# Attention's first query part and one head's rope rows ahead of the other rope copies; second-gate conditioning in the inverse stage, GpSimd out of it

## The chip, the cores and the metric

The kernel runs on one core of one Trainium2 chip. A core has a matrix engine (TensorE, PE in the rows, with its weight loads as PEld), VectorE (DVE), ScalarE (ACT), GpSimd (POOL) and SyncE (SP), which issues most DMA transfers. The metric is the device time of one execution in microseconds (us), as the median of several runs. All times below are microseconds unless a row says ns.

## The reference, cut to what matters

One step of a two-layer diffusion model on 1,024 latent tokens and 128 context tokens with 1,024 channels. Layer 0 mixes with a gated long convolution (Hyena), layer 1 with latent attention of 16 heads. Each layer adds gate * mixer output, and (shift, scale, gate) comes from the conditioning vector.

```python
def adaln(cond, w, b):                      # one call per layer and token group
    m = (jax.nn.silu(cond) @ w + b)[:, None, :]
    return jnp.split(m, 3, axis=-1)         # shift, scale, gate

def hyena_mix(h, ...):                      # layer 0
    proj = h @ w_in
    u = short_conv(proj[..., :3 * HY_WIDTH], conv_w, conv_b)
    gate = proj[..., 3 * HY_WIDTH:]
    x0, x1, v = jnp.split(u, 3, axis=-1)
    z = v * x1
    y = irfft(rfft(z) * hf)[:L]             # hf: the filters' spectrum
    y = (y + z * f_bias) * x0
    return (y * jax.nn.silu(gate)) @ w_out

def mla_latent(h, ...):                     # layer 1, latent tokens
    q_a, kv_a, k_pe, gate = split(h @ w_in)
    q = rmsnorm(q_a) @ w_qb                 # 64 plain and 32 rope columns a head
    ckv = rmsnorm(kv_a)
    q_pe, k_pe = rope(q_pe), rope(k_pe)     # k_pe is shared by all heads
    k_nope, v = split(concat(ckv, ckv_ctx) @ w_kvb)
    p = softmax((q_nope @ k_nope.T + q_pe @ k_pe.T) * scale)
    return ((p @ v) * jax.nn.silu(gate)) @ w_o

xs = xs + g_s * os_                         # the gate of each layer
```

## The kernel before, in words

Everything is fp32 in and out. A product that needs accuracy is made of three matmul passes: each operand is split into a high part (`hi`, a copy into the matmul's own format) and a low part (`lo`, the difference), and high*high, low*high and high*low are added. So `wi_h`/`wi_l`, `lhh`/`lhl` and `kT0`/`kT1` are high and low parts, and an argument of the helper says on which engine each is made.

The program is written stage by stage, and each engine executes its instructions in the order in which they stand in its own list. Blocks under `urgent` are put ahead of work that was written earlier and has not been placed yet; inside `issue_after(last)` work is placed behind a given instruction. The tile framework adds the waits, and a tile that takes over the space of an earlier one waits for that tile's readers. All transfers called on `nc.sync` are issued in order by SP, so one that waits holds up those behind it.

**The inverse stage.** The latent convolution is done by a discrete Fourier transform in eight groups of 128 channels. The inverse transforms (`inverse(g)`) read the spectra of each group with four `pi_raw` loads from PS, one `pp_raw` load (the context tokens), combine them on VectorE (`bf<-Z`, `bf<-ds`, `ds<-W`), and let TensorE transform back (line 548, tile `iv_ps`) into `yv`. In the same stage the last input projections run, for the gate path (`gate_group`, line 418, tile `ip_ps`): their weights come by `wi_raw` loads, their high part is made on ScalarE, and their low part `wi_l` on GpSimd. For the groups whose gate is ready, `gate_y` loads the gate (`xg`), multiplies `yv` by it, and the product is stored to YD. A string of steps, PLAN, sets how inverse transforms (I and i) and gate projections (g) are interleaved; I includes `gate_y`. YP and YG list the groups whose two products run on GpSimd. This work lies between 589 and 717 us after the start. Then `w_out` starts: it splits y into `lhh` and `lhl` and multiplies by the output weights (line 619, tile `wo_ps`).

**Conditioning.** `ada_chunk` loads 1 MB of conditioning weights for 256 columns, multiplies eight 128-row pieces with the conditioning vectors in four groups of rows of one PSUM tile, and copies them out on ScalarE (`ada_ev`). `ada_row` adds the four groups with a small product by `sel`, loads the bias row (`ada_row`), adds it on VectorE, and stores the result by a DMA that GpSimd issues, into `gate_rows`. Those of the second layer's gate are four calls, made after the last `mla_gate` and before `attend`, with their tiles in the space of the `mla_gate` weights and silu tiles (`like`). Their result is read at the end, in `mla_out`.

**The entry of attention.** `mla_gate` makes the attention gate with three-pass products and a silu each (`gsil`), and SP stores it. `attend` then makes the tiles `kT0`, `kT1`, `qT` and `Vt` in space that was freed, and fills the rope rows of `kT` for the four heads of a group from `krh`/`krl` by eight DMA copies (line 976), a row block of 64 each. `attention` then makes the key parts for the first pair (`k_proj`, products of line 989, as those of the query parts; the values are made in line 1021), calls `start(0)`, which loads the gate tile `gt` (two DMAs) and `rope_q`, and makes the three query parts. Part 0 holds the rope columns: its products are copied to `rot0`/`rot1` on ScalarE, 32-row blocks are swapped by two DMAs each (`rot<-rot`), and GpSimd multiplies by `rope_q` and writes `qT`. The scores (line 1287) follow.

Of the kernel before, what the change touches and what calls it, by code (L numbers as in the profile page):

```python
# [9 lines left out]
F32 = mybir.dt.float32  # L10
# [7 lines left out]
P = 128  # L18
D = 1024

GATES = (0, None, None, 1, None, None, None, None)
NY = 6
YP, YG = (0, 1), (0, 1, 2, 3, 4)
WT = ((0, 1, 2, 3), (4, 5), (6, 7), (8,))
XB = 4
PLAN = "g2 I0 I1 g3 I2 I3 g4 g5 I4 i5 i6 i7"
WRB = 3
# [11 lines left out]
GB = 2  # L39
HP = (0,)  # L40
W_LO = "dve"
# [34 lines left out]
class K:  # L76
# [27 lines left out]

    def ada_chunk(self, layer, o, n, pool, ps, kk, bufs, like=None):

        pt = ps.tile([P, 512], F32, name="ada_ps", tag=self.ada_tag, bufs=self.nada)[:, 0:n]
        for k in range(0, 8, kk):
            if like:
                w = pool.tile([P, 8, 336], F32, name="ada_w", tag=like, bufs=bufs)[:, :, 0:n]  # L110
            else:
                w = pool.tile([P, kk, n], F32, name="ada_w", tag="ada_w", bufs=bufs)
            self.ada_dma = self.nc.sync.dma_start(w, self.a["ada_w"][layer, o // 256][:, k:k + kk, o % 256:o % 256 + n])
            for i in range(kk):
                g = (k + i) % 4
                self.PE.matmul(pt[32 * g:32 * g + 32, :], self.cond[:, k + i, :], w[:, i, :],
                               start=k + i < 4, stop=k + i >= 4, tile_position=(0, 32 * g))
        ev = pool.tile([P, n], F32, name="ada_ev", tag="gsil" if like else "ada_ev", bufs=2 if kk * n > 1024 else 1)
        self.S.copy(ev, pt)
        return ev  # L120
# [19 lines left out]

    def ada_row(self, layer, gd, o, n, pool, ps, kk, bufs, like=None):

        ev = self.ada_chunk(layer, 2 * D + o, n, pool, ps, kk, bufs, like)
        pt = ps.tile([P, 512], F32, name="ada_ps", tag=self.ada_tag, bufs=self.nada)[:, 0:n]
        self.PE.matmul(pt[0:2, :], self.sel, ev, start=True, stop=True)
        row = pool.tile([P, n], F32, name="ada_row", tag="gsil", bufs=2)[0:2] if like else pool.tile([2, n], F32, name="ada_row", tag="ada_row", bufs=1)
        self.nc.sync.dma_start(row, self.a["ada_gb"][layer:layer + 1, o:o + n].squeeze(0).partition_broadcast(2))
        self.tt(row, row, pt[0:2, :], ALU.add)
        self.nc.gpsimd.dma_start(gd.squeeze(0)[:, o:o + n], row)
# [497 lines left out]
    def hyena(self):  # L647
# [107 lines left out]
        with self.pool("pc", side="right") as pc, self.pool("pb1", 1, side="right") as pool, \  # L755
# [10 lines left out]
            for step in PLAN.split():  # L766
                c, g = step[0], int(step[1])
                if c == "g":
                    with tc.issue_after(last):
                        self.gate_group(g, q)  # L770
                    late.append(g)
                else:
                    with self.urgent():
# [71 lines left out]
    def mla(self, lh, hT, lT, wp, wo, gd, AB):  # L845
# [3 lines left out]
        with self.pool("mcs", space=PSUM) as ps:  # L849
# [8 lines left out]
            with self.pool("mww", side="left") as wpool:  # L858
# [23 lines left out]
                for h in range(1, 4):  # L882
                    self.mla_gate(h, wpool, ps, hT, lT, GD, 2)
                    if h == 1:
                        self.load_kq(m, "wk", 0, "act", "dve")
                        self.load_kq(m, "wq", 0, "act", "dve")

                self.ada_tag, self.nada = "nm_ps", 3
                for o in range(0, D, 256):
                    self.ada_row(1, gd[1], o, 256, wpool, ps, 8, 2, "wm_" + "hl"[o // 256 % 2])  # L890
            lh.release()
# [72 lines left out]
    def attend(self, at, m):  # L964
# [6 lines left out]

        for j in (0, 2):
            r = slice(32 * j, 32 * j + 64)
            for x, y in zip(kT, m["kr"]):
                for i in range(2):
                    nc.sync.dma_start(x[r, j + i, :].bitcast(F32), y[r, :].bitcast(F32))

# [71 lines left out]
    def attention(self, m):  # L1049
# [20 lines left out]
        def now(work):  # L1070
            for g in work:
                for _ in g:
                    pass

        m["fin"] = None
        now(self.k_proj(m, 0, b) for b in range(3))
        cur, work = start(0)
        now(work)
        u = unit(cur, 0)
# [4 lines left out]
        with self.tc.manual_schedule(engines=ordered):  # L1084
            for G in range(4):
                for ci in range(4):
# [21 lines left out]
                    cur = nxt  # L1108
# [386 lines left out]
```

## Time and profile before

| | us |
|---|---|
| median of 3 runs | 1825.76 (1824.81 to 1826.91) |
| the profiled execution | 1825.55 |
| its span | 1823.7 |
| PE busy | 1753.8 (96%), 11,064 matmuls |
| DVE busy | 1256.7 (69%) |
| ACT busy | 1087.5 (60%) |
| POOL busy | 551.7 (30%) |

The profiled execution lies 0.2 below the median, and its span 1.9 below its own time; what lies around the span is taken as unchanged. Shares are of the whole span, over stages with different limits. A row of the timeline gives the start of a group of like instructions, the time from its first start to its last end, engine, line, operation, out<-in with the names of tiles, shape, count, and in brackets how long its engine sat idle before it and what ended that wait. L976 is line 976 of the kernel before. A row of the chain gives start, duration and what the time was spent on: an engine at work, a DMA, or SP's queue (SPq).

### The profile page before, as it was taken

What the parts mean: (1) busy time and instruction counts of PE and PEld (TensorE: products, weight loads), DVE (VectorE), ACT (ScalarE), POOL (GpSimd) and SP (SyncE); (2) the same over time, 40 slices, a digit from 0 to 9 for tenths busy, and PEclk for the clock granted to TensorE, in tenths of its full rate; (3) what the DMA queues carried; (4) which work ended last, traced back from release to release, by engine and by line L of the source; (5) the groups of instructions that cost most, each with busy time, mean ns of one, the idle gap of its engine ahead of it and who ended that gap; (6) DMA issues with size and microseconds to landing.
All of it is one profiled execution on the core that took longest, in us unless ns stands there. A gap on an engine that the chain in (4) does not pass through costs nothing.

```text
span 1823.7 us, 30675 instructions
## 1 busy us (share of the span) xinstructions
PE 1753.8 (96%) x11064; PEld 1575.4 (86%) x11064; DVE 1256.7 (69%) x2518; ACT 1087.5 (60%) x2580; POOL 551.7 (30%) x756
## 2 busy tenths in 40 slices
PE   6999999999999989999999799999999999999898
PEld 4888989989899878889999589999999999998786
DVE  3948787898885897442250387878787888778454
ACT  7655565756664224334451488878887888788332
POOL 2433333433444232331000143433423342344100
PEclk9999999999999989999999899999999999999999
DMA  8233332111133646323133410100000010002541
GB/s 324 91 110 109 112 104 72 50 54 49 57 102 111 204 154 260 129 82 101 43 92 114 127 32 23 39 24 24 28 30 28 20 32 21 25 29 67 185 133 70
DMA packets 98448, 157.87 MB, mean 87 GB/s; under 512 B 11703, under 2 KB 68311, under 8 KB 97016
## 3 DMA queue, kind: packets, MB, share of 16 engines
q1 hardware_dynamic: 95488, 152.51, 25.7%
q10 hardware_dynamic: 2552, 3.39, 0.6%
q8 instruction: 87, 1.43, 0.3%
q14 instruction: 65, 0.53, 0.1%
q0 software_dynamic: 256, 0.02, 0.0%
HBM read 113.89 MB, written 36.73 MB: 83 GB/s over the span
## 4 chain that ended last, share of the span: by engine, by line
PE 78%; DVE 9%; DMA 5%; ACT 3%; issue 3%; POOL 2%; SPq 1%; DVEq 0%; ACTq 0%; POOLq 0%
PE wo_ps L619 18%; PE ip_ps L418 14%; PE wo_ps L1287 12%; PE av_ps L1172 8%; PE nm_ps L1160 7%; PE wo_ps L989 5%; PE df_ps L367 3%; PE iv_ps L548 2%; PE nm_ps L1021 1%; DMA pi_raw<-PS 1%; DMA wi_raw<-w_in 1%; POOL wi_l L96 1%; DVE pr_o L99 1%; DVE mx L1290 1%; DVE cv L102 1%
## 5 line engine op out<-in xcount | busy, mean ns | idle before, releaser
L1287 PE MATMUL wo_ps<-kT,qT 128*128 128x512 f32 (+1 forms) x1152 | 281.2, 374 | 11.2 <-POOL qT L90 7.5
L1294 ACT ACTIVATE prob<-wo_ps,mx 128x512 f32<-128x512 f32 (+1 forms) x384 | 234.5, 619 | 22.7 <-DVE mx L1292 20.9
L1290 DVE TENSOR_REDUCE mx<-wo_ps 128x1 f32<-128x512 f32 (+1 forms) x384 | 213.0, 596 | 33.0 <-PE wo_ps L1287 32.4
L88 ACT ACTIVATE pt_h<-nm_ps 128x512 fp32r<-128x512 f32 x324 | 193.1, 600 | 70.5 <-PE nm_ps L1160 63.2
L1287 PEld LDWEIGHTS wo_ps<-kT,qT 128*128 128x128 f32 x1152 | 189.0, 190 | 46.5 <-ACT prob L1294 13.4
L96 DVE TENSOR_TENSOR pt_l<-nm_ps,pt_h 128x512 fp32r<-128x512 f32 x324 | 210.7, 683 | 13.0 <-ACT pt_h L88 12.9
L1160 PE MATMUL nm_ps<-ident,prob 128*128 128x128 f32 x1280 | 191.4, 272 | 0.0
L96 POOL TENSOR_TENSOR wi_l<-wi_raw,wi_h 128x512 fp32r<-128x512 f32 x64 | 111.8, 1747 | 242.8 <-ACT wi_h L88 234.6
L1160 PEld LDWEIGHTS nm_ps<-ident,prob 128*128 128x128 f32 x1280 | 150.0, 140 | 8.5
L418 PE MATMUL ip_ps<-hT,wi_h 128*128 128x384 f32 x720 | 152.8, 346 | 0.8 <-ACT cv L500 0.8
L418 PE MATMUL ip_ps<-lT,wi_h 128*128 128x384 f32 x720 | 153.2, 342 | 0.0
L418 PE MATMUL ip_ps<-hT,wi_l 128*128 128x384 f32 x720 | 152.1, 343 | 0.0
L1172 PE MATMUL av_ps<-pt_h,Vt 128*128 128x256 f32 x640 | 138.0, 297 | 0.3 <-ACT pt_h L88 0.3
L1172 PE MATMUL av_ps<-pt_l,Vt 128*128 128x256 f32 x640 | 135.5, 293 | 0.3 <-DVE pt_l L96 0.2
L418 PEld LDWEIGHTS ip_ps<-hT,wi_h 128*128 128x128 f32 x720 | 127.2, 191 | 6.3 <-issue 2.1
L418 PEld LDWEIGHTS ip_ps<-hT,wi_l 128*128 128x128 f32 x720 | 126.3, 189 | 6.8 <-issue 3.3
L418 PEld LDWEIGHTS ip_ps<-lT,wi_h 128*128 128x128 f32 x720 | 128.3, 190 | 3.4 <-issue 0.4
L619 PE MATMUL wo_ps<-wm_h,lhh 128*128 128x256 f32 (+1 forms) x432 | 125.8, 295 | 1.6 <-ACT wm_h L88 1.6
L619 PE MATMUL wo_ps<-wm_l,lhh 128*128 128x256 f32 (+1 forms) x432 | 126.9, 294 | 0.1
L619 PE MATMUL wo_ps<-wm_h,lhl 128*128 128x256 f32 (+1 forms) x432 | 127.0, 295 | 0.0
L1184 POOL TENSOR_SCALAR gt<-gt,sm 128x64 f32<-128x64 f32 x128 | 54.9, 443 | 225.2 <-DVE sm L1175 223.9
L99 POOL TENSOR_TENSOR pr<-ev 128x256 f32<-128x256 f32 x72 | 83.8, 1169 | 128.9 <-ACT ev L375 81.0
(338 smaller groups left out, 4096.7 us busy)
## 6 DMA issues: line engine op xcount, KB each, us to landing
wi_raw<-w_in SPq DMA_DIRECT2D x64, 256.0 KB, 2.9
ada_w<-ada_w SPq DMA_DIRECT2D x12, 1024.0 KB, 7.1
ada_w<-ada_w SPq DMA_DIRECT2D x24, 512.0 KB, 3.9
x_in<-xs SPq DMA_DIRECT2D x16, 512.0 KB, 5.9
PS<-pr_o SPq DMA_DIRECT2D x64, 128.0 KB, 1.9
pi_raw<-PS SPq DMA_DIRECT2D x32, 256.0 KB, 4.0
YD<-yv SPq DMA_DIRECT2D x8, 576.0 KB, 3.3
y<-YD SPq DMA_DIRECT2D x8, 576.0 KB, 10.3
```

The costliest lines, as they stand in the source:

```text
L88: self.S.activation(out, src, AF.Copy)
L96: e.tensor_tensor(out, src, hi.bitcast(F32), ALU.subtract)
L99: (eng or self.V).tensor_tensor(out, x, y, op)
L418: mm = self.PE.matmul(pt, w[:, k, :], x[c][:, k, :], start=s == 0 and k == 0, stop=s == 2 and k == 7)
L619: self.PE.matmul(pt, x[k][:, sl], w[:, k, :], start=s == 0 and k == 0, stop=s == 2 and k == kt - 1)
L989: self.PE.matmul(pt[:, :n], x[:, k, o:o + P], y[:, k, c], start=s == 0 and k == 0, stop=s == 2 and k == kt - 1)
L1160: self.PE.transpose(pt[:, P * i:P * i + P], u["p"][i % 2][n // 2][:, P * (2 * (n % 2) + i // 2):P * (2 * (n % 2) + i // 2) + P], self.ident)
L1172: self.PE.matmul(u["po"][:, :256], m["V"][:, 2 * n + e, j, :], u[n][1 + s][:, 256 * e:256 * e + 256], start=n == first and e + s == 0, sto ...
L1184: self.G.tensor_scalar(o, o, u["sm"][:, i, 3:4], None, ALU.mult)
L1287: self.PE.matmul(pt[:, :n], x[:, j, P * i:P * i + P], y[:, j, o:o + n], start=s == 0, stop=s == 2)
L1290: self.V.tensor_reduce(mx[:, b:b + 1], c["s", i, b][:, :n], AX.X, ALU.max)
L1294: self.S.activation(c["p"][i][b], c["s", i, b][:, :n], AF.Exp, bias=c["mx"][i][:, 3:4], accum_out=c["sm"][:, i, b:b + 1])
```

## The change

Four things are done. The second layer's gate conditioning (the four `ada_row` calls) moves from the space between `mla_gate` and `attend` into PLAN, as the steps a0 to a3, with tiles of the inverse stage's own pool, and the option `like` goes. The lists YP, YG and HP become empty: the five products `yv*xg`, two low parts `lhl` and one high part `lhh` that GpSimd made are now made by VectorE (the `lhh` by ScalarE). In `attend` the rope rows of head 0 (j=0) are written by a VectorE cast (kT1 by ScalarE), and the other three by DMA copies: six instead of eight. In `attention`, `start(0)` and query part 0 are issued under `urgent`, ahead of the first keys in the code.

```diff
-YP, YG = (0, 1), (0, 1, 2, 3, 4)
+YP, YG = (), ()
-PLAN = "g2 I0 I1 g3 I2 I3 g4 g5 I4 i5 i6 i7"
+PLAN = "g2 I0 a0 I1 g3 I2 a1 I3 g4 a2 g5 I4 a3 i5 i6 i7"
-HP = (0,)
+HP = ()
...
-    def ada_chunk(self, layer, o, n, pool, ps, kk, bufs, like=None):
+    def ada_chunk(self, layer, o, n, pool, ps, kk, bufs):
...
-            if like:
-                w = pool.tile([P, 8, 336], F32, name="ada_w", tag=like, bufs=bufs)[:, :, 0:n]
-            else:
-                w = pool.tile([P, kk, n], F32, name="ada_w", tag="ada_w", bufs=bufs)
+            w = pool.tile([P, kk, n], F32, name="ada_w", tag="ada_w", bufs=bufs)
...
@@ inverse stage
+                elif c == "a":
+                    self.ada_row(1, gd[1], 256 * g, 256, pool, ps, 8, 2)
...
@@ mla(), after the last mla_gate
-                self.ada_tag, self.nada = "nm_ps", 3
-                for o in range(0, D, 256):
-                    self.ada_row(1, gd[1], o, 256, wpool, ps, 8, 2, "wm_" + "hl"[o // 256 % 2])
...
@@ attend()
-        for j in (0, 2):
-            r = slice(32 * j, 32 * j + 64)
-            for x, y in zip(kT, m["kr"]):
-                for i in range(2):
-                    nc.sync.dma_start(x[r, j + i, :].bitcast(F32), y[r, :].bitcast(F32))
+        for j in (0, 2, 1, 3):
+            r = slice(64 * (j // 2), 64 * (j // 2) + 64)
+            for i, (x, y) in enumerate(zip(kT, m["kr"])):
+                x, y = x[r, j, :], y[r, :].bitcast(F32)
+                if j:
+                    nc.sync.dma_start(x.bitcast(F32), y)
+                elif i:
+                    self.S.copy(x, y)
+                else:
+                    self.V.tensor_copy(x, y)
...
@@ attention()
+        with self.urgent():
+            cur, work = start(0)
+            now(work[:1])
         now(self.k_proj(m, 0, b) for b in range(3))
-        cur, work = start(0)
-        now(work)
+        now(work[1:])
```

SP's list at the entry of attention, before. `ada_w` and `ada_row` are the loads of the last second-gate chunks, `krh` and `krl` the split rope rows, `gate0` and `gate1` the stored attention gate, `rot0` the first half of query part 0:

```order
L113 DMA ada_w_10319<-ada_w 128x8x256
L147 DMA ada_row_10295<-ada_gb 2x256
L147 DMA ada_row_10314<-ada_gb 2x256
L147 DMA ada_row_10333<-ada_gb 2x256
L147 DMA ada_row_10352<-ada_gb 2x256
L976 DMA kT0_10361<-krh_9350 64x1408 x2
L976 DMA kT1_10362<-krl_9351 64x1408 x2
...
L1061 DMA gt_10413<-gate0_7332 128x256
L1061 DMA gt_10413<-gate1_7333 128x256
L1063 DMA rope_q_10416<-rope_q 128x256
L1042 DMA rot0_10428<-rot0_10428 32x256 x2
```

The "..." stands for the second set of four copies. The same place on SP in the changed kernel, from the last two gate stores on; the "..." stands for the second and third pair of copies:

```order
L957 DMA gate7_7415<-gsil_10325 128x256
L957 DMA gate8_7416<-gsil_10353 128x256
L972 DMA kT0_10361<-krh_9426 64x1408
L972 DMA kT1_10362<-krl_9427 64x1408
...
L1061 DMA gt_10380<-gate0_7408 128x256
L1061 DMA gt_10380<-gate1_7409 128x256
L1063 DMA rope_q_10383<-rope_q 128x256
L1042 DMA rot0_10395<-rot0_10395 32x256 x2
```

The conditioning loads have left the place, the copies stand directly behind the last gate store, two copies are gone, and the gate tile, `rope_q` and the swaps are still behind all copies.

SP's list in the inverse stage, before, from the third group's loads on (PS2 and PS3 are the spectra of groups 2 and 3, XG1 the gate of group 1, YD0 the product of group 0):

```order
L591 DMA pp_raw_6151<-PP2_90 128x256
L402 DMA wi_raw_7048<-w_in 128x512
L544 DMA pi_raw_6095<-PS2_82 128x2x256
L544 DMA pi_raw_6103<-PS2_82 128x2x256
L544 DMA pi_raw_6111<-PS2_82 128x2x256
L544 DMA pi_raw_6119<-PS2_82 128x2x256
L591 DMA pp_raw_6219<-PP3_91 128x256
L599 DMA xg_5901<-XG1_97 128x1152
L778 DMA YD0_104<-yv_5803 128x1152
L544 DMA pi_raw_6163<-PS3_83 128x2x256
```

The same place in the changed kernel:

```order
L588 DMA pp_raw_6170<-PP2_90 128x256
L110 DMA ada_w_6454<-ada_w 128x2048
L541 DMA pi_raw_6114<-PS2_82 128x2x256
L399 DMA wi_raw_7124<-w_in 128x512
L541 DMA pi_raw_6122<-PS2_82 128x2x256
L144 DMA ada_row_6194<-ada_gb 2x256
L541 DMA pi_raw_6130<-PS2_82 128x2x256
L777 DMA YD0_104<-yv_5803 128x1152
L596 DMA xg_5920<-XG1_97 128x1152
L541 DMA pi_raw_6138<-PS2_82 128x2x256
L588 DMA pp_raw_6257<-PP3_91 128x256
L110 DMA ada_w_6728<-ada_w 128x2048
```

A 1 MB load of conditioning weights stands ahead of the third group's spectra, the bias row's load between them, and the store of group 0 and the gate load of group 1 have moved ahead of that group's last load.

GpSimd's list over the inverse stage, before (`yv` with its gate `xg`, the low parts `wi_l` of the last gate projections, and `lhh`/`lhl` of the output projection):

```order
L96 TENSOR_TENSOR wi_l_6953<-wi_raw_6958,wi_h_6952 128x512
L99 TENSOR_TENSOR yv_5803<-yv_5803,xg_5833 128x1152
L99 TENSOR_TENSOR yv_5871<-yv_5871,xg_5901 128x1152
L99 TENSOR_TENSOR yv_6126<-yv_6126,xg_6156 128x1152
L99 TENSOR_TENSOR yv_6194<-yv_6194,xg_6224 128x1152
L96 TENSOR_TENSOR wi_l_7047<-wi_raw_7048,wi_h_7046 128x512
...
L99 TENSOR_TENSOR yv_6636<-yv_6636,xg_6666 128x1152
...
L90 TENSOR_SCALAR lhh0_7296<-y0_6874 128x1152
L96 TENSOR_TENSOR lhl0_7297<-y0_6874,lhh0_7296 128x1152
L96 TENSOR_TENSOR lhl1_7301<-y1_6875,lhh1_7300 128x1152
```

And in the changed kernel:

```order
L96 TENSOR_TENSOR wi_l_7029<-wi_raw_7034,wi_h_7028 128x512
L146 DMA gate_rows1_907<-ada_row_5852 2x256
L146 DMA gate_rows1_907<-ada_row_6194 2x256
L146 DMA gate_rows1_907<-ada_row_6468 2x256
L96 TENSOR_TENSOR wi_l_7123<-wi_raw_7124,wi_h_7122 128x512
L96 TENSOR_TENSOR wi_l_7123<-wi_raw_7128,wi_h_7122 128x512
L146 DMA gate_rows1_907<-ada_row_6742 2x256
L96 TENSOR_TENSOR wi_l_7216<-wi_raw_7217,wi_h_7215 128x512
```

The five products and three splits are gone from GpSimd; the `wi_l` splits stay, and the four stores of conditioning rows stand among them.

## Rows read from the trace of the kernel before

**Rows 1.** The page's chain that ended last, share of the span by engine.

```profile
PE 78%; DVE 9%; DMA 5%; ACT 3%; issue 3%; POOL 2%; SPq 1%; DVEq 0%; ACTq 0%; POOLq 0%
```

**Rows 2.** Windows: stretch, sum, PE PEld DVE ACT POOL busy, PEclk, DMA share, GB/s.

```profile
1030.00:1040.00 10.00, 4.85 (x12) 3.56 (x12) 2.05 (x4) 0.00 (x0) 5.90 (x10) 0.55 0.32 94
```

**Rows 3.** Timeline of all engines from 995 us on, the last gate store.

```profile
1000.19 0.61 SPq L962 DMA_DIRECT2D gate<-gsil  x1
```

**Rows 4.** The chain in order of time, 1000 to 1060 us.

```profile
1000.63 4.40 PE wo_ps L989 x21
...
1014.16 0.55 SPq L976
...
1020.27 2.15 SPq L976
...
1022.46 1.52 SPq L976
...
1030.65 2.05 DMA rot<-rot
...
1040.88 1.32 PE wo_ps L1287 x6
```

**Rows 5.** Timeline of PE, 1012 to 1056 us.

```profile
1011.64 1.11 PE L116 MATMUL ada_ps<-ada_w,cond 128*32 128x256 f32 x13
...
1013.78 0.51 PE L1021 MATMUL nm_ps<-wk_h,ckh 128*128 128x256 f32 x2
...
1017.00 0.62 PE L989 MATMUL wo_ps<-qnh,wq_h 128*128 128x256 f32 x3 [0.33 <-DVE kT L96]
...
1034.13 4.85 PE L1287 MATMUL wo_ps<-kT,qT 128*128 128x512 f32 x12 [7.50 <-POOL qT L90]
```

**Rows 6.** Timeline of DVE, 596 to 732 us.

```profile
608.96 3.19 DVE L99 TENSOR_TENSOR bf<-Z 128x256 f32<-128x256 f32 x2
...
660.61 4.12 DVE L99 TENSOR_TENSOR bf<-ds 128x256 f32<-128x256 f32 x2
...
667.31 0.76 DVE L99 TENSOR_TENSOR bf<-Z 128x256 f32<-128x256 f32 x2
...
670.33 1.83 DVE L99 TENSOR_TENSOR ds<-W 128x768 f32<-128x768 f32 x2 [2.26 <-ACT W L549]
...
718.87 1.35 DVE L96 TENSOR_TENSOR lhl<-y,lhh 128x1152 fp32r<-128x1152 f32 x1
```

**Rows 7.** Timeline of POOL, 596 to 732 us.

```profile
608.98 2.88 POOL L99 TENSOR_TENSOR yv<-yv,xg 128x1152 f32<-128x1152 f32 x1 [7.62 <-ACT yv L594]
...
652.30 9.40 POOL L96 TENSOR_TENSOR wi_l<-wi_raw,wi_h 128x512 fp32r<-128x512 f32 x1 [6.45 <-ACT wi_h L88]
...
702.47 2.10 POOL L90 TENSOR_SCALAR lhh<-y 128x1152 fp32r<-128x1152 f32 x1 [8.60 <-PE ip_ps L418]
```

**Rows 8.** Timeline of PE, 638 to 735 us.

```profile
665.92 3.75 PE L548 MATMUL iv_ps<-ic,pi_raw 128*128 128x256 f32 x8 [5.00 <-DMA pi_raw<-PS]
...
717.66 0.50 PE L619 MATMUL wo_ps<-wo_h,lhl 128*128 128x512 f32 x1 [1.51 <-DVE lhl L96]
```

**Rows 9.** Timeline of ACT, 596 to 732 us.

```profile
716.38 1.16 ACT L88 ACTIVATE lhh<-y 128x1152 fp32r<-128x1152 f32 x1 [0.88 <-DVE y L99]
```

**Rows 10.** The chain in order of time, 590 to 735 us.

```profile
681.20 29.51 PE ip_ps L418 x170
```

**Rows 11.** Tile ada_ps: count: duration ns min/median/max, first and last start us, forms.

```profile
L145 PE MATMUL ada_ps<-ada_ev,sel x16: 377/378/378, 95.7 to 1013.5; 128*2 128x256 f32 x16
```

**Rows 12.** Tile ada_row, the columns as above.

```profile
L99 DVE TENSOR_TENSOR ada_row<-ada_row,ada_ps x8: 396/404/409, 96.4 to 1015.2; 2x256 f32<-2x256 f32 x8
L149 POOL DMA_DIRECT2D gate_rows<-ada_row x8: 518/552/756, 97.5 to 1015.9; - x8
...
DMA to landing us min/median/max: 1.6/3.1/4.6
```

**Rows 13.** The DMA view, 595 to 690 us.

```profile
DMA packets 10476, 15.61 MB, mean 164 GB/s; under 512 B 787, under 2 KB 8523, under 8 KB 10468
```

## What the change should do: the prediction

> **What bounds the kernel now.** I read the page first: the chain of work that ended last is TensorE for 78% [rows 1], so an edit is worth what it takes out of the stretches in which TensorE waits. The windows show two such stretches where the diff works: the inverse stage (about 590 to 717 us) and the entry of attention (1000 to 1046 us).
>
> At the entry, the store behind the last gate silu is issued at 1000.19 for 0.61 [rows 3]. The first score matmul starts at 1034.13, after 7.50 us in which TensorE waits for a GpSimd row of qT [rows 5]. The chain in order of time says why: it runs through the queue of SP. The first kT copy goes out at 1014.16, the seventh of eight at 1022.46, then gt, rope_q and the rot swaps follow, and the first swaps land at 1032.70, 2.05 after 1030.65 [rows 4]. The wait also costs clock: the granted clock is 0.55 of full in 1030 to 1040 [rows 2], the lower of its two levels, 1.2 GHz, for most of it, after TensorE had stood still from 1026.63, which is 1034.13 less 7.50.
>
> In the inverse stage VectorE is nearly full, and GpSimd gets in its way. Each GpSimd product yv*xg takes 2.88 [rows 7], and the VectorE pair bf<-Z that runs beside it takes 3.19 where the same pair alone takes 0.76 [rows 6]. The other way round, one wi_l split on GpSimd takes 9.40 beside a dense VectorE [rows 7]. SP issues in order, so the next w_in load and the pi_raw loads behind it are late, TensorE stands 5.00 for pi_raw [rows 8], and VectorE 2.26 for W [rows 6].
>
> **The change, part by part.**
>
> *Entry: second-gate conditioning gone, copies earlier and fewer.* Before, the first kT copy waited for the last second-gate row, which lies in the same space as the attention tiles. Now only the last gate store stands ahead of the copies in SP, and their latest wait is the last gate matmul, which reads the space that kT takes. That store went out at 1000.19 and took 0.61 [rows 3]; nine matmuls of the first query part now stand ahead of it on TensorE; three of them took 0.62 [rows 5], overlapped with the next three, so I take 1.4 for nine. The first copy then starts at 1000.19 + 0.61 + 1.4 = 1002.2.
>
> From first copy to first score it was 1034.13 - 1014.16 = 19.97 [rows 4, 5]. Two of eight copies become casts. The early copies cost SP 0.55 each, the later ones 1.52 to 2.15 [rows 4]; two fewer are worth 1.1 to 4.3, and I take 3.6, since the missing two shorten the full queue and not its start. The first score comes at 1002.2 + 19.97 - 3.6 = 1018.6, 15.5 earlier. With the two bounds it is 13.0 to 16.2.
>
> The rot swaps are still behind all six copies in SP's order, whatever the order in the code says, so I book nothing for that. The earlier query matmuls are not what the swaps wait for either.
>
> What could cover this: the key, value and other query parts. They took 4.40 from 1000.63 on [rows 4] and then the time from 1013.78 to 1026.63 [rows 5], so 4.4 + 12.85 = 17.25, and from 1000.63 on they end at about 1017.9, just before the first score. The two casts are not in the trace. A VectorE split of 1152 columns takes 1.35 [rows 6] and a ScalarE copy of 1152 takes 1.16 [rows 9]; by columns, 1408 give 1.6 and 1.4. Between nothing (both run while TensorE still has matmuls) and 1.4 (they delay every eviction behind them) I take nothing, and keep the 1.4. A shorter wait may also keep the clock up: twelve scores took 4.85 after it [rows 5] and six took 1.32 a little later [rows 4], so 2.2 could come back. I book 0 and keep 2.2 for the low end. Entry: **-15.5**, from -11.6 to -18.4.
>
> *Inverse stage, VectorE.* Four pairs like the one above lose 3.20 - 0.76 = 2.44 each, and a fifth block is 4.12 in place of 0.76 [rows 6]: 9.8 + 3.4 = 13.2 relieved. Added are five products at the 1.35 of a 1152-column operation, 6.8, and four row additions at 0.40, 1.6 [rows 6, 12]. Net -4.8.
>
> *Inverse stage, TensorE.* Four conditioning chunks come in: eight matmuls of two passes each, of which thirteen took 1.11 [rows 5], and a sel product of 0.38 [rows 11], so about 1.5 each and 6.0 in all. They lie in this stage's idle time (the 5.00 and some 3 more); without that cover the 6.0 are paid. The order also moves the last inverse matmul ahead of 24 in-projection matmuls: 194 instead of 170 follow it. 170 take 29.51 [rows 10], so 24 take 4.2. If the inverse stage is tied to VectorE, the end of the in-projections moves by -4.8 + 4.2 = -0.6. If the 5.00 stall goes as well, by -5.6. The stall came from a starved wi_l, and VectorE gets no less dense, so I take half: **-3.1**, from -7 to +6.
>
> *Its waits.* Each ada_row load in SP waits for the gate_rows store of the row before. Behind the second of them queue two pi_raw loads, the store of y0 and a gate load; TensorE's inverse matmuls wait for those. Such small transfers take 1.6 to 4.6 to land [rows 12], and pi_raw is loaded about seven us ahead, so I book nothing.
>
> The Trainium skill (SBUF — State Buffer, the "DVE blocks DMA" trap) speaks against this placement: a DMA issued from GpSimd needs GpSimd to write descriptors, and a VectorE operation that holds the shared port pair keeps it from that, about 3.1 us for 0.62 by its figures. By that the three waits would cost up to 7.5 where I book 0; the rows here, 0.52 to 0.76 to issue, show no such wait, though the first-gate rows ran beside a less dense VectorE.
>
> *Output projection.* lhh0 goes from GpSimd, where it was made at 702.47 [rows 7], before the in-projections ended, to ScalarE behind the last silu: 0.8 + 1.16 [rows 9] = 1.9 of waiting. The 1.51 wait for lhl [rows 8] goes, since no GpSimd split runs beside VectorE any more. **+0.4**, from -1.5 to +3 (two more splits of 1.35 ahead of the others).
>
> **Sum.** -15.5 - 3.1 + 0.4 = -18.2. The profiled execution took 1825.55 (span 1823.7), 0.2 below the median 1825.76, so 1807.3; I say 1807.
>
> **The rivals.**
> 1. *The inverse stage pays in full.* VectorE gets its 8.4 and no relief, because the remaining wi_l splits keep blocking it. For it: 9.40 for a single split. Against it: 3.19 and 0.76 side by side. 1825.55 - 15.5 + 8.4 + 0.4 = 1819.
> 2. *Both stalls go.* -15.5 - 2.2 - 7 + 0.4 = -24.3, so 1801. For it: both are traced to one queue. Against it: VectorE stays dense.
> 3. *Slower: the loads pace the inverse stage.* Four loads of 1 MB enter SP's queue ahead of pi_raw. If the stage keeps its 164 GB/s [rows 13], 4.2 MB more take 25.6, and the time is 1825.55 - 15.5 + 25.6 = 1836. It ends slower from 19.2 on (15.5 + 3.7). Against it: the queue is half idle there, 15.61 MB in 95 us.
> 4. *It doesn't do what it says.* The copies start no earlier, because another reader holds their space; two copies fewer are left: -3.6, 1822.
> 5. *The stores on GpSimd starve.* The small transfers take 4.6 instead of 1.6 [rows 12], three times, and SP passes that on: 1807.3 + 9 = 1816. This is the mechanism of the page named above.
>
> **How the numbers follow.** My forecast has 56%, with a range of its own of 1802 to 1813; rival 1 has 16%, rival 2 14%, rival 3 7%, rival 4 4%, rival 5 3%. The range 1799 to 1819 takes in the forecast, rivals 1, 2 and 5, and leaves out rivals 3 and 4 and the tails. A measurement of this kernel tells 0.2%, 3.7 us, from no change: faster than that 0.91 (all but rival 3 and half of rival 4), within it 0.02, slower 0.07.
>
> **What would show it.** Right: the first kT copy within 2 us of 1002 less what the inverse stage gained, the first score some 17 us after it, TensorE waiting at most 3 us for qT; bf<-Z at 0.76; in-projections ending 3 us earlier. Wrong: a first copy that waits for GpSimd; pi_raw or ada_w as the releaser of inverse matmuls for more than 5 us together; a wi_l of several us with pi_raw behind it; the first score waiting for the casts. The prediction falls if the inverse stage gets longer by more than 8 us, or if the swaps no longer end the entry.

## The result and the profile after

The changed kernel takes 1803.5 us as the median of its first four runs (1801.83 to 1809.27), against 1826.27 for the kernel before: a ratio of 0.9884, 95% interval 0.9865 to 0.9903. Six more runs of it (e1 below) gave 1805.97 (1803.63 to 1812.44), a ratio of 0.9902 (0.9887 to 0.9917). So it is faster by some 20 to 23; 1807 was forecast, and the range of 1799 to 1819 holds it. The profiled execution took 1801.83, with a span of 1799.7.

The page's chain by engine, of the changed kernel, to be read beside [rows 1]:

```profile
PE 75%; DVE 11%; DMA 4%; ACT 4%; issue 3%; POOL 2%; SPq 0%; ACTq 0%; DVEq 0%; POOLq 0%
```

SP's queue is down from 1% to 0% of the chain. At the entry, the timeline of SP of the changed kernel (beside [rows 3, 4]):

```profile
989.81 7.07 SPq L957 DMA_DIRECT2D gate<-gsil  x3
996.98 0.54 SPq L972 DMA_DIRECT2D kT<-krh  x1
...
1001.29 1.67 SPq L972 DMA_DIRECT2D kT<-krh  x1
1003.00 1.52 SPq L972 DMA_DIRECT2D kT<-krl  x1
1004.56 2.74 SPq L1061 DMA_DIRECT2D gt<-gate  x2
1007.36 0.46 SPq L1063 DMA_DIRECT2D rope_q<-rope_q  x1
1007.92 3.09 SPq L1042 DMA_DIRECT2D rot<-rot  x4
```

The first copy leaves at 996.98 instead of 1014.16, directly behind the gate stores, and the swaps at 1007.92. The chain reaches the swaps here over TensorE's value parts and not over SP's copies; but SP issues transfer behind transfer from 996.98 to 1011.01, and e7 below tests which of the two holds the swaps. The timeline of PE there, then of DVE, and of ACT (beside [rows 5]):

```profile
1013.71 2.69 PE L1289 MATMUL wo_ps<-kT,qT 128*128 128x512 f32 x12 [3.48 <-POOL qT L90]
```

```profile
994.20 0.89 DVE L976 CAST kT<-krh 64x1408 fp32r<-64x1408 f32 x1 [36.66 <-PE wo_ps L616]
```

```profile
996.43 1.35 ACT L974 CAST kT<-krl 64x1408 fp32r<-64x1408 f32 x1
```

The wait for qT has halved, from 7.50 to 3.48, and is not gone: the swaps still end the entry. The twelve scores behind it take 2.69 instead of 4.85. The two casts take 0.89 and 1.35, and TensorE has no other wait between the last gate matmul and the first score.

In the inverse stage, TensorE's waits in the kernel before (the lines view of 590 to 711: busy time and mean, then the idle time before the group and what ended it), and the windows of the kernel before and then of the changed one (columns as in [rows 2]):

```profile
L548 PE MATMUL iv_ps<-ic,pi_raw 128*128 128x256 f32 x254 | 61.7, 396 | 8.2 <-DMA pi_raw<-PS 6.1 <-ACT W L549 2.0 <-ACT u L436 0.2
```

```profile
640.00:660.00 20.00, 17.87 (x80) 15.61 (x80) 19.86 (x39) 6.06 (x12) 12.01 (x3) 0.91 0.44 144
660.00:680.00 20.00, 15.00 (x66) 13.16 (x65) 16.19 (x34) 3.85 (x8) 4.45 (x2) 0.83 0.50 168
```

```profile
640.00:660.00 20.00, 20.00 (x105) 15.63 (x104) 19.10 (x41) 7.22 (x16) 1.27 (x1) 1.00 0.64 210
660.00:680.00 20.00, 20.00 (x111) 19.09 (x111) 19.14 (x46) 4.94 (x10) 7.74 (x2) 1.00 0.28 97
```

TensorE is busy without a gap, and the clock that fell to 0.91 and 0.83 behind its waits stays at 1.00. The timelines of DVE and of POOL in the changed kernel answer to [rows 6, 7, 12]:

```profile
604.54 0.76 DVE L99 TENSOR_TENSOR bf<-Z 128x256 f32<-128x256 f32 x2
605.22 1.35 DVE L99 TENSOR_TENSOR yv<-yv,xg 128x1152 f32<-128x1152 f32 x1
```

```profile
616.17 0.52 POOL L146 DMA_DIRECT2D gate_rows<-ada_row  x1 [12.42 <-DVE ada_row L99]
...
660.67 7.25 POOL L96 TENSOR_TENSOR wi_l<-wi_raw,wi_h 128x512 fp32r<-128x512 f32 x1 [3.99 <-ACT wi_h L88]
```

The product costs VectorE 1.35, and `bf<-Z` beside it is back at 0.76. One `wi_l` is still stretched to 7.25, and no TensorE wait follows from it.

**Where the time is.** The profiles below reach the end of the forward transforms at 573.2 to 580.3, without order by kernel, and take 128.9 to 133.1 from the last score to the end, both in parts that the change doesn't touch. So I compare stages by the distance between marks that the tile views give: the last start of a forward transform's matmul (tile df_ps), of an in-projection (ip_ps), the first of an attention-gate matmul (wm_h,lhh of wo_ps), the first and the last score (kT,qT of wo_ps). For the changed kernel two of these rows read:

```profile
L616 PE MATMUL wo_ps<-wm_h,lhh x432: 276/282/422, 813.1 to 995.5; 128*128 128x256 f32 x96, 128*128 128x336 f32 x48
...
L1289 PE MATMUL wo_ps<-kT,qT x1152: 274/393/792, 1013.7 to 1668.7; 128*128 128x512 f32 x129, 128*128 128x256 f32 x63
```

813.1 to 1013.7 is a distance of 200.6. The table has all runs that follow; the names are those of the experiments below.

| run | transforms to in-projections | to first gate matmul | to first score | first to last score | median | ratio (95%) |
|---|---|---|---|---|---|---|
| before | 133.7 | 108.0 | 215.7 | 657.0 | 1826.27 | 1 |
| changed | 130.9 | 108.2 | 200.6 | 655.0 | 1803.5 | 0.9884 (0.9865 to 0.9903) |
| e1 changed again | 130.9 | 108.2 | 200.2 | 657.6 | 1805.97 | 0.9902 (0.9887 to 0.9917) |
| e2 GpSimd back | 131.4 | 110.8 | 200.8 | 656.3 | 1808.93 | 0.9918 (0.9897 to 0.9939) |
| e3 conditioning back | 120.4 | 113.3 | 216.1 | 659.1 | 1816.39 | 0.9948 (0.9936 to 0.996) |
| e4 before, GpSimd out | 120.4 | 113.4 | 218.7 | 657.6 | 1818.57 | 0.9963 (0.9951 to 0.9974) |
| e5 eight copies | 131.1 | 108.2 | 203.8 | 656.7 | 1809.07 | 0.9899 (0.9877 to 0.9921) |
| e6 query part late | 131.0 | 108.1 | 198.6 | 655.9 | 1805.15 | 0.9874 (0.9854 to 0.9894) |
| e7 swaps ahead | 131.0 | 109.8 | 191.0 | 659.7 | 1798.87 | 0.9838 (0.982 to 0.9857) |
| e8 lhh0 back | 130.9 | 107.8 | 200.2 | 656.4 | 1804.17 | 0.9874 (0.9854 to 0.9894) |
| e9 before, conditioning moved | 131.3 | 119.2 | 204.2 | 656.5 | 1813.72 | 0.9943 (0.9921 to 0.9965) |
| e10 no conditioning product | 120.4 | 114.0 | 199.8 | 656.0 | 1801.29 | 0.9865 (0.9841 to 0.989) |
| e11 swaps ahead, query late | 130.9 | 108.2 | 198.5 | 658.5 | 1803.95 | 0.9884 (0.9862 to 0.9906) |
| e12 conditioning bunched | 131.3 | 108.2 | 199.1 | 657.6 | 1806.36 | 0.9894 (0.9873 to 0.9915) |

Ratios are to the kernel before on the same chip: e1 to e4 ran on one, e5 to e8 on another, e9 to e12 on a third.

The change makes -2.8 in the inverse stage, +0.2 at the output projection and -15.1 at the entry, together -17.7. The medians differ by 20 to 23; the remaining 2 to 5 lie in no stage that the change touches. Each row of the table is one profiled execution; where the code of a stage is the same, the first four columns still differ by up to 0.2, 8.4, 3.0 and 4.1.

### The profile page after: what moved, and what is told of

Same layout as the page of the kernel before. It is cut to its first block, busy times and chain, and to the rows that moved or that the text cites. A ratio compares the mean times of both kernels' runs of the same rounds, so it can differ in the third digit from the quotient of the medians.

```text
span 1799.7 us, 30649 instructions
## 1 busy us (share of the span) xinstructions
PE 1747.2 (97%) x11064; PEld 1568.3 (87%) x11064; DVE 1249.6 (69%) x2526; ACT 1088.1 (60%) x2582; POOL 528.1 (29%) x748
## 4 chain that ended last, share of the span: by engine, by line
PE 75%; DVE 11%; DMA 4%; ACT 4%; issue 3%; POOL 2%; SPq 0%; ACTq 0%; DVEq 0%; POOLq 0%
PE wo_ps L616 18%; PE wo_ps L1289 12%; PE ip_ps L415 11%; PE av_ps L1174 8%; PE nm_ps L1162 7%; PE wo_ps L989 5%; PE iv_ps L545 3%; PE df_ps L364 2%; DMA wi_raw<-w_in 2%; PE nm_ps L1021 1%; DVE pr_o L99 1%; DVE cv L102 1%; PE ada_ps L113 1%; POOL wi_l L96 1%; DVE mx L1292 1%
## 5 line engine op out<-in xcount | busy, mean ns | idle before, releaser
L1296 ACT ACTIVATE prob<-wo_ps,mx 128x512 f32<-128x512 f32 (+1 forms) x384 | 234.0, 618 | 17.9 <-DVE mx L1294 16.0
L96 DVE TENSOR_TENSOR pt_l<-nm_ps,pt_h 128x512 fp32r<-128x512 f32 x324 | 210.5, 682 | 13.2 <-ACT pt_h L88 13.1
```

The source lines that it names most:

```text
L96: e.tensor_tensor(out, src, hi.bitcast(F32), ALU.subtract)
L1296: self.S.activation(c["p"][i][b], c["s", i, b][:, :n], AF.Exp, bias=c["mx"][i][:, 3:4], accum_out=c["sm"][:, i, b:b + 1])
```

## The experiments

**e1.** The changed kernel again, unedited.

> The changed kernel once more, unchanged, so that the others have a neighbour on the same chip and its scatter is known (its first four runs lay between 1801.83 and 1809.27). Every theory expects 1803, within 3, and the stages where its first profile has them: in-projections end at 705.25, first score at 1013.7.

It repeats the stages to 0.4. Its last column but two also says that the 2.0 which the first profile gained between the scores (655.0 against 657.0) is scatter: here it is 657.6.

**e2. GpSimd gets its work back.**

```diff
-YP, YG = (), ()
+YP, YG = (0, 1), (0, 1, 2, 3, 4)
-HP = ()
+HP = (0,)
```

> The changed kernel with the three lists restored: five products, two low parts and one high part on GpSimd again. Theory (the products on GpSimd and VectorE's operations stretch each other, and that made the two stalls of TensorE): bf<-Z beside a product is at 3.2 again, TensorE waits for pi_raw again by some 5 us, the in-projections end 5 to 10 later than 705.25, the whole is 1808 to 1813. Rival (the stalls went because the store of the product and the gate load now stand ahead of the last spectrum load in SP's list): bf<-Z is at 3.2 but the in-projections end within 2 of 705.25, and the whole is 1802 to 1805.

The timeline of DVE, then of PE:

```profile
625.61 3.19 DVE L99 TENSOR_TENSOR bf<-Z 128x256 f32<-128x256 f32 x2
```

```profile
712.48 0.50 PE L616 MATMUL wo_ps<-wo_h,lhl 128*128 128x512 f32 x1 [1.79 <-DVE lhl L96]
713.75 0.50 PE L616 MATMUL wo_ps<-wo_h,lhl 128*128 128x512 f32 x1 [0.30 <-DVE lhl L96]
```

(The row at 625.61 is one of five pairs at 2.87 to 3.22.) My theory fell: `bf<-Z` is stretched again, and yet the in-projections end where they did (131.4 against 130.9) and TensorE never waits in the stage. What the rival forecast holds there; the cause that it names, the order in SP's list, isn't shown by it, and the whole, 1808.93, is above its 1802 to 1805. The loss of 2.6 is at the output projection, where TensorE waits for `lhl`. The profiled execution is the fastest of the six (1803.54 to 1816.83), so 2.6 need not be the usual loss.

**e3. The conditioning back at the entry,** with all the rest of the change: the four `ada_row` calls stand after the last `mla_gate` and the steps a0 to a3 are out of PLAN.

```diff
-PLAN = "g2 I0 a0 I1 g3 I2 a1 I3 g4 a2 g5 I4 a3 i5 i6 i7"
+PLAN = "g2 I0 I1 g3 I2 I3 g4 g5 I4 i5 i6 i7"
...
+                self.ada_tag, self.nada = "nm_ps", 3
+                for o in range(0, D, 256):
+                    self.ada_row(1, gd[1], o, 256, wpool, ps, 8, 2, "wm_" + "hl"[o // 256 % 2])
```

> The changed kernel with the second-gate conditioning back between the attention gate and attend. Theory (its matmuls, 8 us of TensorE, are paid wherever they stand, since TensorE never idles in the inverse stage of the changed kernel; at the entry they cost what SP's copies wait for): in-projections end up to 8 earlier (697 to 700), the first copy goes 11 to 12 later against the start of the attention gate, and the whole is +4 to +8, 1807 to 1811. Rival (the conditioning lies free in the inverse stage, which VectorE paces): in-projections end within 2 of 705.25 and the whole is +12 to +15, 1815 to 1818.

The timeline of PE, then a window; the last row is the same wait in the changed kernel:

```profile
701.72 0.80 PE L619 MATMUL wo_ps<-wo_h,lhh 128*128 128x512 f32 x1 [4.17 <-ACT lhh L88]
```

```profile
700.00:710.00 10.00, 8.28 (x24) 6.44 (x25) 9.62 (x11) 8.62 (x11) 0.00 (x0) 0.66 0.98 390
```

```profile
706.92 0.50 PE L616 MATMUL wo_ps<-wo_h,lhh 128*128 128x512 f32 x1 [1.69 <-ACT lhh L88]
```

The conditioning isn't free in the stage: without it the in-projections end 10.5 earlier. But 5.1 of that is given back at once, since TensorE then waits 4.17 for the first `lhh` (1.69 in the changed kernel) and works at the lower clock behind it (0.66 in this window). At the entry it costs 216.1 - 200.6 = 15.5. So -10.5 + 5.1 + 15.5 = +10.1, and the medians of e3 and e1 differ by 10.4: between my theory, which missed what is given back, and its rival. The timeline of SP has the first copy at 1009.80, which is 199.3 behind the first gate matmul (195.8 in the kernel before), and the first score comes 16.79 after it, as in the changed kernel.

**e4. The kernel before with the lists empty,** the edit of e2 the other way round.

> The kernel before with the three lists empty and nothing else. Theory (GpSimd's products made the stalls): both stalls of TensorE go (8.2 us of waiting and the lower clock after them), in-projections end at 697 to 702 instead of 710.7, the wait for lhh costs 1.7, the entry is as before, and the whole is 1814 to 1819. Rival of the prediction (VectorE gets 8.4 us more and is no faster, since the wi_l splits still block it): in-projections end at 709 to 713 and the whole is 1824 to 1828.

```profile
700.76 0.79 PE L619 MATMUL wo_ps<-wo_h,lhh 128*128 128x512 f32 x1 [4.35 <-ACT lhh L88]
```

This row is from the timeline of PE. GpSimd's share alone is worth 13.3 in the inverse stage, not the 13.2 - 6.8 = 6.4 by which I had VectorE relieved: no wait of TensorE is left there. That is what the stalls cost before, 8.2 of waiting for pi_raw, W and u, and 133.7 - 8.2 - 120.4 = 5.1 of the same work done slower, for which the lower clock of the two windows shown above gives about 20 * 0.09 + 20 * 0.17 = 5.2. The output projection gives back 5.4 by the 4.35 wait for `lhh`. The entry of this profile is 3.0 longer with nothing changed in it; 2.8 of that lie ahead of the first copy (at 1008.05 in SP's timeline, 198.6 behind the first gate matmul), where the conditioning still stands. With it the stages leave -4.9, without it -7.9, of the -7.4 that the medians show; the profiled execution is 2.1 above its median.

**e5. Eight DMA copies again,** no casts.

```diff
...
-                if j:
-                    nc.sync.dma_start(x.bitcast(F32), y)
-                elif i:
-                    self.S.copy(x, y)
-                else:
-                    self.V.tensor_copy(x, y)
+                for i in range(2):
+                    nc.sync.dma_start(x[r, j + i, :].bitcast(F32), y[r, :].bitcast(F32))
```

> The changed kernel with all eight rope copies as DMAs, as before (no casts). Theory (SP's list sets the first score): two more copies at 1.2 to 1.8 each, so the first score comes 2.5 to 3.6 later against the last gate matmul (20.4 to 21.5 instead of 17.9), and the whole is +3, 1807 to 1810. Rival (something else sets it, the value parts on TensorE or the copies of rot on ScalarE): within 0.7 of 17.9, and the whole is within 2 of the changed kernel.

```profile
1016.60 4.79 PE L1284 MATMUL wo_ps<-kT,qT 128*128 128x512 f32 x12 [7.03 <-POOL qT L90]
```

The timeline of PE has the first score 21.5 after the last gate matmul (995.1) instead of 17.9, and the wait for qT at 7.03 again. The distance to the first score grows by 3.2 to 3.6, and the whole is 3.9 above e6 and 4.9 above e8 on the same chip, whose stages are those of the changed kernel; by the ratio it can't be told from e1. In the stage, the two casts are worth what two DMAs cost in SP's queue.

**e6. The query part after the keys again.**

```diff
-        with self.urgent():
-            cur, work = start(0)
-            now(work[:1])
         now(self.k_proj(m, 0, b) for b in range(3))
-        now(work[1:])
+        cur, work = start(0)
+        now(work)
```

> The changed kernel without the early query part: keys first, then start(0) and all three query parts, as before. Theory of the prediction (the swaps stand behind the six copies in SP's list either way): first score within 1 of the changed kernel's distance from the last gate matmul plus the 1.1 us of nine matmuls that come after it now, so 18 to 20, and the whole within 2 of the changed kernel. Rival (the early part is what lets the swaps be ready): rot is copied later than SP gets to it, the first score comes 3 or more later, the whole is +3 to +5.

The first score stands 17.9 behind the last gate matmul, as with the early part, the wait for qT is 2.37, and the whole is not above the changed kernel's. The "first queries ahead" of this change are worth nothing: their nine matmuls are made earlier, and the swaps wait for SP. The distance from the first gate matmul to the first score is, if anything, shorter without them: 198.6 against 199.1 to 200.8 in the six runs that have them, the casts and no conditioning at the entry.

**e7. The swaps really ahead.** The gate tile, `rope_q` and `rot` get a small pool of their own, and the six copies, now in `rope_copies`, are issued behind query part 0. The lines that are replaced are left out.

```diff
+                with self.pool("aw0") as p0, ExitStack() as es:
+                    m["p0"] = p0
+                    gen = self.attention(m)
+                    next(gen)
+                    self.rope_copies(m)
+                    k4p.release()
+                    m["pool"] = es.enter_context(self.pool("aw"))
...
             cur, work = start(0)
             now(work[:1])
+        yield None
```

> The changed kernel with the gate tile, rope_q and the rot swaps really ahead of the six remaining copies in SP's list (their tiles in a small pool of their own, which is there before the copies' source is released). Theory (those copies are what the first score waits for, and heads 2, 1 and 3 need their rows later): TensorE's wait of 3.5 for qT goes to under 1, the first score comes some 3 earlier, when the value parts are done, and the whole is -3 to -4 against the changed kernel. Rival (the copies are needed at once by the second head): the 3 us come back as a wait of the second score group, and the whole is within 1.5 of the changed kernel.

The timelines of SP and of PE:

```profile
1000.28 0.88 SPq L1064 DMA_DIRECT2D gt<-gate  x2
1001.20 0.42 SPq L1066 DMA_DIRECT2D rope_q<-rope_q  x1
1001.73 2.50 SPq L1045 DMA_DIRECT2D rot<-rot  x4
1004.33 0.52 SPq L979 DMA_DIRECT2D kT<-krh  x1
...
1010.35 1.51 SPq L979 DMA_DIRECT2D kT<-krl  x1
```

```profile
1007.31 0.63 PE L1294 MATMUL wo_ps<-kT,qT 128*128 128x512 f32 x2
...
1016.15 0.50 PE L1024 MATMUL nm_ps<-wk_h,ckh 128*128 128x256 f32 x2 [1.24 <-DVE Vt L97]
```

The wait for qT is gone. The first score comes 8.2 after the last gate matmul, among the value parts, which now follow it. The whole is 1798.87, a ratio of 0.9838, whose interval lies below both of the changed kernel's, and 6.3 and 5.3 below e6 and e8 on the same chip: the fastest version here, 27 to 30 below the kernel before. Not all of the 9.2 to 9.6 by which the first score comes earlier stays: from the first to the last score it takes 659.7, 2 to 5 more than in the changed kernel's two profiles, and the output projection, which this edit doesn't touch, 1.6 more.

**e8. One split back to GpSimd:** `HP = (0,)`.

> The changed kernel with one split given back to GpSimd: the first high part, lhh0. Theory (it is the wait of 1.7 at the start of the output projection): the wait goes, the output projection starts 1.5 to 1.7 earlier, the whole is -1 to -2 against the changed kernel. Rival (the wait moves to the first low part, or the weights' splits on VectorE are slowed by it): within 0.7 of the changed kernel.

```profile
710.34 0.50 PE L616 MATMUL wo_ps<-wo_h,lhl 128*128 128x512 f32 x1 [1.35 <-DVE lhl L96]
```

The rival holds: the timeline of PE has a wait of 1.35 for `lhl` in place of the 1.69 for `lhh`, and the stage is 107.8 instead of 108.2.

**e9. The kernel before with the conditioning moved,** and nothing else: the edit of e3 the other way round.

> The kernel before with the conditioning steps in the inverse stage and nothing else (GpSimd keeps its products and splits; eight copies; keys first). Theory (the stalls of TensorE in the inverse stage go by either part alone: the conditioning's matmuls lie where TensorE waited, and the run with GpSimd's work back in the changed kernel had no such wait): no TensorE wait over 1 us between 590 and 700, the in-projections end within 2 of the changed kernel (703 to 707), the first score comes some 21 after the last gate matmul, and the whole is 1808 to 1813. Rival (with GpSimd in it the stage still stalls, and pays the conditioning on top): in-projections at 712 to 719, the whole 1818 or more.

The timelines of PE, POOL and DVE:

```profile
721.53 0.79 PE L616 MATMUL wo_ps<-wo_h,lhl 128*128 128x512 f32 x1 [10.61 <-POOL lhl L96]
```

```profile
707.98 13.49 POOL L96 TENSOR_TENSOR lhl<-y,lhh 128x1152 fp32r<-128x1152 f32 x1 [4.82 <-ACT lhh L88]
```

```profile
709.51 7.69 DVE L96 TENSOR_TENSOR lhl<-y,lhh 128x1152 fp32r<-128x1152 f32 x6
717.12 1.88 DVE L96 TENSOR_TENSOR wo_l<-w_raw,wo_h 128x512 fp32r<-128x512 f32 x3
```

In the inverse stage the theory holds: TensorE never waits, and the distance is 131.3, so the conditioning lies where the stalls were and gains 2.4. What I hadn't expected is the output projection, 11.2 longer: one GpSimd split is held for 13.49 beside a row of VectorE splits, and TensorE waits 10.61 for it. The code there is that of e2, where the same split took 2.84 and the distance was 110.8, so this is a matter of timing and not of every execution. The stages of this profile make -2.4 + 11.2 - 11.5 = -2.7, and the medians differ by 11.8: the profiled execution is 3.2 above its median, and 5.9 more lie in stages that the edit doesn't touch.

**e10. No conditioning product:** the gate rows get the bias alone, so the outputs lack that part of the gate. The loads of its weights go with it.

```diff
-                    self.ada_row(1, gd[1], 256 * g, 256, pool, ps, 8, 2)
+                    row = pool.tile([2, 256], F32, name="ada_row", tag="ada_row", bufs=1)
+                    nc.sync.dma_start(row, a["ada_gb"][1:2, 256 * g:256 * g + 256].squeeze(0).partition_broadcast(2))
+                    nc.gpsimd.dma_start(gd[1].squeeze(0)[:, 256 * g:256 * g + 256], row)
```

> The changed kernel without the second gate's conditioning product: the gate rows hold the bias alone, its weights are not loaded and its 36 matmuls not made. Theory (TensorE never waits in the changed inverse stage, so the work is paid in full there): in-projections end 7 to 9 earlier, but the wait for lhh grows from 1.7 to about 4.2 and the clock dips there, as in the two runs without conditioning in the stage, so the output projection gives back 3 to 5 and the whole is -3 to -6 against the changed kernel. Rival (it lies in free time): in-projections within 2, the whole within 2.

```profile
706.46 0.80 PE L616 MATMUL wo_ps<-wo_h,lhh 128*128 128x512 f32 x1 [5.44 <-ACT lhh L88]
```

In-projections 10.5 earlier, as in e3 and e4, then a 5.44 wait (timeline of PE) and 5.8 given back, net -4.7; its neighbour e12 has a median 5.1 higher. So of the conditioning the changed kernel pays about 5; where it was, it cost 11.5 (e9) to 15.5 (e3) at the entry. Of the 10.5, TensorE's own work is 8.9: the lines view of the changed kernel, 590 to 707, has

```profile
L113 PE MATMUL ada_ps<-ada_w,cond 128*32 128x256 f32 x64 | 6.5, 389 | 0.0
...
L142 PE MATMUL ada_ps<-ada_ev,sel 128*2 128x256 f32 x8 | 2.4, 378 | 0.0
```

**e11. Swaps ahead, but the query part after the keys:** e7 with the edit of e6.

> The faster version with the swaps ahead of the copies, but keys first and the query part after them. Theory (the early query part is worth nothing behind the copies, and much once SP is free for the swaps: rot is then ready when SP gets to it): the swaps fall behind five of six copies again, the first score comes 15 to 18 after the last gate matmul instead of 8.2, and the whole is +5 to +7 against that version, as the changed kernel. Rival (only the list of SP counts, and the gate tile and rope_q ahead are most of it): first score at 9 to 12, the whole within 2 of that version.

```profile
1011.61 2.57 PE L1293 MATMUL wo_ps<-kT,qT 128*128 128x512 f32 x8 [2.83 <-POOL qT L91]
```

In the timeline of PE the first score is 16.9 behind the last gate matmul (994.7), and the median is 5.1 above that of e7, on another chip. The timeline of SP has five of the six copies ahead of the swaps again. So the early part is worth nothing behind the copies and some 5 once SP is free for its swaps.

**e12. The four steps behind one another:** `PLAN = "g2 I0 I1 g3 I2 I3 g4 g5 I4 a0 a1 a2 a3 i5 i6 i7"`.

> The changed kernel with the four conditioning steps behind one another after the fifth inverse transform instead of spread over the stage. Theory (it is 8 us of TensorE's time wherever it stands): in-projections end within 2 of the changed kernel, the whole within 2. Rival (spread out, the weight loads of 1 MB hold nothing up; bunched, they hold up the spectra and each ada_row waits for the store before it): TensorE waits 3 or more in the stage and the whole is +3 to +8.

131.3 against 130.9, no wait of TensorE in the stage, and 1806.36: no difference. Between these two orders, where in the stage the work stands doesn't matter.

## Why the prediction was right

**Entry, -15.5 forecast, -15.1 measured.** Both steps come out. From the first gate matmul to the first copy it was 1014.16 - 818.4 = 195.8 and is 996.98 - 813.1 = 183.9, so -11.9 where the step from 1014.16 to 1002.2 gave -12.0. From first copy to first score it was 19.97 and is 16.73, so -3.2 for the -3.6 that I took; e5 gives the same by itself. Of it all, e9 shows -11.5 without casts or an early query part, and e6 shows that the latter, booked at nothing, brings nothing. That the sum is met to 0.4 is in part luck: with the same code the entry took 215.7 in the kernel before and 218.7 in e4, as the conditioning ended earlier or later. "TensorE waiting at most 3 us for qT" was slightly missed, with 3.48. The 2.2 kept for the clock came in the first profile, where the twelve scores took 2.69 for 4.85, and not in e1, where they took 4.85 again (timeline of PE).

**Inverse stage, -3.1 forecast, -2.8 measured, by two terms that were each far off.** The step that failed is *Inverse stage, VectorE* together with the sentence that the conditioning's 6.0 "lie in this stage's idle time". I sized GpSimd's removal by the operations that it relieves, -13.2 + 6.8 = -6.4 on VectorE (-4.8 with the four row additions); alone it is -13.3 (e4), because it ends the stalls and the slower work behind them, 8.2 and 5.1. And with the stalls gone no idle time is left, so the conditioning is paid: +10.5 (e3, e10), more than my 6.0. The 6.0 was also added up too low: by its own rows a chunk is 16 * 1.11 / 13 + 0.38 = 1.7, and [rows 11] has two products by `sel` for each, 16 for eight; measured it is 6.5 + 2.4 = 8.9. Rival 2 was right that both stalls go. The 4.2 for the order of the in-projections was not measured apart; with 8.9 of the +10.5 in the conditioning's own matmuls, 1.6 are left for it at most. The half-way value of -3.1 hit the sum of -13.3 and +10.5 by luck. The two parts are no sum of their own either: the conditioning alone is -2.4 in the stage (e9), since it fills the same stalls. Why it ends them with GpSimd's products still there, by more ready work for TensorE or by the loads' other order in SP's list, was not separated.

**Output projection, +0.4 forecast, +0.2 measured.** The wait for `lhh` is 1.69 for the 1.9 worked out, and the 1.51 for `lhl` is gone. What the sum didn't see is that this place is a floor: whoever ends the in-projections 10 earlier gets 5 of it back as a longer wait for `lhh` (e3, e4, e10), and whoever leaves the splits on GpSimd may wait 10.61 (e9). So with the conditioning moved, emptying GpSimd's lists is worth nothing in the stage where its products stood, and in the two executions profiled 2.6 (e2, the fastest of its runs) and 11.0 (e9) here; in the whole, e2 can't be told from e1.

**The rivals.** Rival 1 (VectorE stays blocked) fell with `bf<-Z` at 0.76. Rival 3 (loads pace the stage) fell with no wait of TensorE for pi_raw. Rival 4 fell with the first copy. Rival 5 fell: the stores issue in 0.52 to 0.57 and land after 3.1 in the median (DMA view), and TensorE waits for none of it. So the Trainium skill's "DVE blocks DMA" trap (SBUF — State Buffer) doesn't show in these rows. The Trainium skill ties it there to VectorE operations in a 2-port mode, as an fp32 copy, and excepts TENSOR_TENSOR, which is what VectorE does beside the store at 616.17 (a product from 615.81 for 1.34, timeline of DVE); the prediction had applied the trap too widely.

The Trainium skill's rule on the same page that the port pair is an exclusive lock, held for the whole instruction by whoever starts first while the other blocks, fits e2, whose timelines of POOL and DVE have a split of 2.84 and beside it a VectorE pair of 3.92 that takes 1.42 in e9:

```profile
706.83 2.84 POOL L96 TENSOR_TENSOR lhl<-y,lhh 128x1152 fp32r<-128x1152 f32 x1 [4.60 <-ACT lhh L88]
```

```profile
705.91 3.92 DVE L99 TENSOR_TENSOR cv<-cv 128x1024 f32<-128x1024 f32 x2
```

It does not by itself give e9's 13.49. There VectorE goes through a dozen operations at its usual pace until 717.12 + 1.88 = 719.00, and the split ends 2.47 later, so it looks held out by the whole row and not by one instruction. That the lock is the cause was not tested by itself.

**What stays open.** 2 to 5 of the measured gain lie in no stage that was changed. How often a split on GpSimd is held as in e9 is not shown, since each run has one profile.

## What to carry to other kernels

Work that fills a stall and work that removes it don't add up: price the second with the first in place, by leaving one part out, and look at the next stage for what it gives back. Code written "ahead" is ahead only on the engine that one looks at; read the queue of the engine that ends the wait, here SP's, where moving seven shorter transfers ahead of six long ones brought a further 5 to 6 (e7), and only with the query part made early (e11). And a sum that comes out right can rest on two terms that are wrong by 7 and by 10.

## What the runs showed of the hardware

A GpSimd split of 128x1152 took 2.84 in e2, where a VectorE pair beside it took 3.92 in place of 1.42, and 13.49 in e9, where VectorE worked on at its usual pace until 2.47 before the split's end.

A wait of TensorE cost more than its length: where it stood for 4.17 and 4.35 (e3, e4) the granted clock of 700 to 710 was 0.66 and 0.68, and the output projection gave back 5.1 and 5.4. Waits of about one length were not followed by the same clock: behind 1.69 in the changed kernel it was 1.00 in 700 to 710, and behind 1.79 and 0.30 in e2 it was 0.83 in 710 to 720; and the twelve scores behind a wait of 3.48 to 3.53 took 2.69 in the changed kernel, 4.85 in e1 and 4.10 in e8.
